# Moving key norms, token shift, decay mask and weight high parts between VectorE, ScalarE and TensorE in a two-layer trunk kernel

## The chip, the cores and the metric

One core of one Trainium2 chip runs the kernel. The metric is the device time of one execution in microseconds (us). Lower is better.

## The reference

A trunk of two layers over 512 tokens of width 1024, in fp32. Each layer is a mixer and then a SwiGLU feed-forward network (FFN), both behind an RMS norm and added to the residual stream. The first mixer ("even") has a short gated convolution and a gated delta rule with six heads of 128; the second ("odd") has an RWKV-7 scan with eight heads of 64, beside latent attention with eight heads. What the change touches is this:

```python
# even: gated delta rule in chunks
g = jnp.cumsum(to_chunks(g), axis=-1)
diff = g[..., :, None] - g[..., None, :]
decay = jnp.where(causal, jnp.exp(jnp.where(causal, diff, 0.0)), 0.0)
L = jnp.where(strict, jnp.einsum('bhncd,bhnsd->bhncs', kb, k) * decay, 0.0)
Tm = unit_lower_inverse(L)
...
# odd: token shift, key norm, RWKV-7 scan
z_rwkv = z + mu * (token_shift(z) - z)
r, k, v, wd, ad, gd = split_cols(z_rwkv, RWKV_SPLITS)
kk = l2_normalize((k * k_k).reshape(hshape))
k = k * (1.0 + (a - 1.0) * k_a)
y = rwkv7_scan(r_h, decay, k_h, v_h, kk, a)
```

## The kernel before

The order of the work is: even mixer (0 to about 267 us), its FFN (to 674), odd mixer (to 993), its FFN (to 1380). Activations lie with channels on the 128 partitions and the 512 tokens along the free dimension, in tiles of 128x512.

**Products.** To reach fp32 accuracy, weights and activations are split into a high part rounded to fp32r and a low part, and each product is three fp32r matmuls of 128x128 by 128x512. One projection of 1024 channels onto 128 is thus 24 matmuls into one PSUM bank. `weight` (line 340) loads a piece of a weight matrix, makes the high part (`hi`, by `self.copy`) and the low part (`lo`, raw minus high). A trace names these tiles `w`.

**Order of the work.** The program is a set of generators, one for each head, projection or convolution. A planner (`Plan`, `Engine`, `Core.run`) runs them against estimated costs and writes one instruction list for each engine; the chip then runs each list in its order. `self.copy` is put on ScalarE or VectorE and `E` on VectorE or GpSimd, whichever the planner expects to be done first. `A` is always ScalarE, `V` VectorE, `PE` TensorE. A generator takes a PSUM bank with `take("mx")` and gives it back with `rel("mx")`; the tags are `mx` (trace: mxps), `mm` (mmps) and `sc` (scps).

**Even mixer.** `even` projects queries, keys and values, convolves them with four taps (in the trace `x2k<-mmps,rs`, then one tap on ScalarE and three on VectorE, `conv_qkv`) and computes the gates: `gc`, the running sum of the log decay, and `gl`, its total. `decay(h)` makes for each head the mask matrix `dm` = exp(min(running sum - gc, mask)) of four chunks: four small matmuls of a broadcast gate column with the triangular `incl` put the running sums into a bank (trace: `mxps<-incl,g`), four VectorE instructions subtract `gc` and take the minimum with `negm` (0 or very negative), and ScalarE takes the exponential of all four, and that of the bank for `qT`. Each head's key product (`kT`) gives the squared key norms, through GpSimd (`R`) and VectorE (`rinv`), and then the matrix `L`. When all six heads have it, a blocked triangular inverse follows, mostly in series on VectorE (tile `big`), and then the scan over chunks on TensorE.

**Odd mixer.** `shifted(i, out)` (line 1260) multiplies a projection's bank by the RMS factor `rs` into `z`, gives the bank back, scales `z` by `omm` = 1 - mu and adds mu times `z` one token earlier. `keys(j)` (line 1504) serves two heads at a time, j = 0 to 3. It builds `ar[j]` (keys times decay, the first column of each 64-token chunk copied apart by VectorE, `ar<-x2k 128x8`) and `bk[j]`. The norms are summed on TensorE into `rn`, 128x8, by `TENSOR_SCALAR` and `RECIPROCAL`; VectorE copies `rn` out to 128x512 (`rb`, trace `x2k<-rn`) and four transposes put it into a bank, by which `kk0` is multiplied. Elsewhere `bk` is multiplied by `pcol`, and a blocked inverse like that of the even mixer works on tile `mem`. Attention follows, with its queries read back from memory (`f<-qd`), among early projections of the FFN.

Of the kernel before, what the change touches and what calls it, by code (L numbers as in the profile page):

```python
# [11 lines left out]
AF = mybir.ActivationFunctionType  # L12
# [4 lines left out]
T = 512  # L17
# [235 lines left out]
class Core:  # L253
# [86 lines left out]
    def weight(self, src, kt, m):  # L340

        n = kt * m
        part = lambda dt=F32R: self.tile(self.low, [128, 512], dt, "w", 12, typed=True)
        out = []
        for a in range(0, n, 512):
            w = min(512, n - a)
            if isinstance(src, tuple):
                hi, lo = part(), part()
                for t, x in zip((hi, lo), src):
                    self.dma(t[:, :w].bitcast(F32), x[:, a:a + w])  # L350
            else:
                raw, hi, lo = part(F32), part(), part()
                self.dma(raw[:, :w], src[:, a:a + w])
                self.copy(hi[:, :w], raw[:, :w])
                self.E.tensor_tensor(lo[:, :w], raw[:, :w], hi[:, :w], op=OP.subtract)
            out += [(hi[:, i:i + m], lo[:, i:i + m]) for i in range(0, w, m)]
        return out
# [170 lines left out]
    def rel(self, tag="mm"):  # L528
        self.held[tag] -= 1
# [138 lines left out]
    def even(self, gain, consts):  # L668
# [5 lines left out]
        with ExitStack() as ctx:  # L674
# [20 lines left out]
            betaf, gf = (t.rearrange("p h n -> p (h n)") for t in (beta, g))  # L695
            gc, gl = tl([U], "gc"), tl([U], "gl")
            neg_eg, e_gl, e_kd = tl([U], "neg_eg"), tl([U], "e_gl"), tl([U], "e_kd")
# [52 lines left out]
            def gates():  # L750
# [29 lines left out]
                PE.matmul(pg[:, U:2 * U], self.ones, gf, start=True, stop=True)  # L780
                V.tensor_copy(gc, pg[:, 0:U])
                V.tensor_copy(gl, pg[:, U:2 * U])
                rel("mx")
# [7 lines left out]
            def decay(h):  # L791
# [3 lines left out]
                for n in range(N):  # L795
                    u = h * N + n
                    PE.matmul(pb[:, blk(n)], gf[:, u:u + 1].to_broadcast([128, 128]), incl, start=True, stop=True)
                for n in range(N):
                    u = h * N + n
                    V.scalar_tensor_tensor(dm[:, u], pb[:, blk(n)], gc[:, u:u + 1], negm, op0=OP.subtract, op1=OP.min)  # L800
                A.activation(dm[:, h * N:(h + 1) * N], dm[:, h * N:(h + 1) * N], AF.Exp)
                A.activation(qT[:, h], pb, AF.Exp)
                rel("mx")
# [397 lines left out]
    def odd(self, xs, old, out):  # L1201
# [5 lines left out]
        with ExitStack() as ctx:  # L1207
# [52 lines left out]
            def shifted(i, out, ps=None, tag="mm"):  # L1260
# [4 lines left out]
                V.memset(z[:, 0:1], 0.0)  # L1265
                V.tensor_tensor(z[:, 1:T + 1], ps, rs, op=OP.mult)
                rel(tag)
                t = tmp()
                self.copy(t, z[:, 1:T + 1], omm[:, i:i + 1])
                V.scalar_tensor_tensor(out, z[:, 0:T], mu[:, i:i + 1], t, op0=OP.mult, op1=OP.add)  # L1270

# [232 lines left out]
            def keys(j):  # L1504
# [17 lines left out]
                E.tensor_tensor(ar[j][:, :, 0, 1:], ca[:, :, 1:], cE[:, :, 0:63], op=OP.mult)  # L1522
                V.tensor_copy(ar[j][:, :, 0, 0:1], ca[:, :, 0:1])
                V.scalar_tensor_tensor(kk0, th, 1.0, kk0, op0=OP.add, op1=OP.mult)
# [16 lines left out]
                V.reciprocal(rn, rn)  # L1541
                rb = tmp()
                V.tensor_copy(rb.rearrange("p (a c) -> p a c", c=64), rn[:, :, None].to_broadcast([128, 8, 64]))
                yield rb
                p = yield from take("mx")
                for n in range(4):
                    PE.transpose(p[:, blk(n)], rb[:, blk(n)], ident)
                V.tensor_tensor(kk0, kk0, p, op=OP.mult)
# [423 lines left out]
```

## Time and profile before

| what | value |
|---|---|
| median of three runs | 1370.57 us (1367.95 to 1374.75) |
| profiled execution, its own time | 1381.73 us |
| span of the profiled execution | 1380.0 us |
| TensorE busy | 1342.4 us (97%), 7526 records |
| VectorE busy | 850.9 us (62%) |
| ScalarE busy | 520.2 us (38%) |
| GpSimd busy | 365.6 us (26%) |
| chain of waits that ended last | TensorE 82%, VectorE 11%, DMA 3% |
| mean granted TensorE clock | 0.986 |

In the profile, PE is TensorE, DVE VectorE, ACT ScalarE and POOL GpSimd. One fp32r matmul is one record; an fp32 matmul is two records. The shares are means over stages that have different limits, so a stage's own stretch has to be looked at. The profiled execution took 0.8% more than the median.

### The profile page before, as it was taken

Reading aid. Unit: us, or ns where it says so; the run is one execution under the profiler, and the core shown is the slowest. Engines: PE = TensorE matmul, PEld = TensorE weight load, DVE = VectorE, ACT = ScalarE, POOL = GpSimd, SP = SyncE. Lnnn points to the kernel's source line nnn. Section 1 sums busy time; section 2 is a strip of 40 time slices with the busy share of each in tenths; the row PEclk is TensorE's granted clock in tenths of the full one; section 3 lists DMA queues with packets and bytes.
Section 4 is the critical chain, followed back from the end, with each engine's and each line's share of the span. In section 5 each row is a group of like instructions: output and inputs, shape, how many; then the busy total and the mean of one; then the engine's idle time right before and its main releaser. Section 6 shows DMA issues by size and latency. Waiting matters only on the chain.

```text
span 1380.0 us, 20285 instructions
## 1 busy us (share of the span) xinstructions
PE 1342.4 (97%) x7526; PEld 1080.5 (78%) x7526; DVE 850.9 (62%) x1598; ACT 520.2 (38%) x976; POOL 365.6 (26%) x367
## 2 busy tenths in 40 slices
PE   8988999999999999999989999999999999999998
PEld 5876888888887888888866777766788888888887
DVE  6999678657676555444398965656665443344432
ACT  5444464243233233334233144626544332233321
POOL 4454143225777766001122301430030000000000
PEclk9999899999999999999999999999999999999999
DMA  4222111256888987334623422475342333333332
GB/s 151 70 69 72 37 47 62 91 161 219 312 321 302 323 265 254 100 95 139 208 92 138 155 94 93 114 215 184 108 145 92 100 95 92 104 97 95 97 116 92
DMA packets 99939, 193.78 MB, mean 140 GB/s; under 512 B 13056, under 2 KB 21248, under 8 KB 99840
## 3 DMA queue, kind: packets, MB, share of 16 engines
q1 hardware_dynamic: 86976, 146.87, 33.5%
q0 software_dynamic: 12864, 45.62, 9.2%
q8 instruction: 59, 0.97, 0.3%
q14 instruction: 40, 0.33, 0.1%
HBM read 151.55 MB, written 40.89 MB: 139 GB/s over the span
## 4 chain that ended last, share of the span: by engine, by line
PE 82%; DVE 11%; DMA 3%; ACT 2%; issue 1%; POOL 1%; SPq 0%; DVEq 0%; POOLq 0%; ACTq 0%
PE mfps L390 56%; PE mmps L390 12%; PE mxps L390 10%; DVE x2k L242 3%; DVE big L242 3%; PE scps L390 2%; PE mxps L394 2%; DVE mem L242 1%; DVE ar L242 1%; DVE f L242 1%; DVE bk L242 1%; ACT mem L242 1%; DMA w<-in_w_oo 1%; DVE w L242 1%; SPq L318 0%
## 5 line engine op out<-in xcount | busy, mean ns | idle before, releaser
L390 PE MATMUL mfps<-big,w 128*128 128x512 f32 x3168 | 725.9, 389 | 0.0
L390 PEld LDWEIGHTS mfps<-big,w 128*128 128x128 f32 x3168 | 594.3, 188 | 123.7 <-DVE big L242 0.4
L242 DVE TENSOR_TENSOR w<-w,w 128x512 fp32r<-128x512 f32 (+1 forms) x318 | 253.4, 797 | 335.7 <-ACT w L242 325.7
L242 ACT ACTIVATE w<-w 128x512 fp32r<-128x512 f32 (+1 forms) x343 | 212.6, 621 | 462.1 <-DMA w<-in_w_gu 172.1
L390 PE MATMUL mmps<-big,w 128*128 128x512 f32 x936 | 246.9, 410 | 0.6 <-DVE x2k L242 0.6
L390 PEld LDWEIGHTS mmps<-big,w 128*128 128x128 f32 x936 | 172.4, 193 | 43.8 <-issue 7.0
L242 POOL TENSOR_TENSOR sqacc<-x2k,sqacc 128x512 f32<-128x512 f32 x21 | 28.1, 1339 | 236.8 <-ACT x2k L242 236.8
L242 POOL TENSOR_TENSOR slo<-sraw,shi 128x1024 fp32r<-128x1024 f32 (+1 forms) x36 | 74.2, 2062 | 14.6 <-DMA w_odl<-slo 12.3
L390 PE MATMUL mfps<-hid,w 128*128 128x512 f32 x288 | 71.6, 389 | 1.7 <-DVE hid L242 1.7
L390 PE MATMUL mxps<-big,w 128*128 128x512 f32 x288 | 73.2, 399 | 0.0
L242 POOL TENSOR_TENSOR w<-w,w 128x512 fp32r<-128x512 f32 x38 | 50.0, 1317 | 71.7 <-ACT w L242 38.2
L390 PEld LDWEIGHTS mfps<-hid,w 128*128 128x128 f32 x288 | 54.0, 188 | 13.4 <-DVE hid L242 2.2
L242 ACT ACTIVATE x2k<-x2k 128x512 f32<-128x512 f32 x61 | 38.5, 631 | 65.5 <-DVE x2k L242 52.2
L242 DVE TENSOR_TENSOR x2k<-mfps,rs 128x512 f32<-128x512 f32 x88 | 59.9, 683 | 3.1 <-PE mfps L390 2.6
L390 PEld LDWEIGHTS mxps<-big,w 128*128 128x128 f32 x288 | 52.2, 188 | 10.1 <-issue 0.2
L242 POOL CAST shi<-sraw 128x1024 fp32r<-128x1024 f32 (+1 forms) x36 | 35.2, 979 | 46.4 <-DMA w_odh<-shi 13.8
L242 DVE TENSOR_TENSOR x2k<-x2k,x2k 128x512 f32<-128x512 f32 x52 | 41.4, 798 | 4.6 <-ACT x2k L242 3.0
L394 PE MATMUL mxps<-c_ident,x2k 128*128 128x128 f32 (+1 forms) x182 | 31.2, 283 | 12.9 <-DVE x2k L242 9.8
L394 PEld LDWEIGHTS mxps<-c_ident,x2k 128*128 128x128 f32 (+1 forms) x182 | 20.8, 139 | 28.2 <-DVE x2k L242 16.7
L242 DVE TENSOR_TENSOR xres<-mfps,xres 128x512 f32<-128x512 f32 x32 | 22.0, 689 | 32.0 <-PE mfps L390 31.9
L242 ACT ACTIVATE x2k<-mxps 128x512 f32<-128x512 f32 (+4 forms) x60 | 26.5, 457 | 31.9 <-PE mxps L390 16.9
L242 DVE TENSOR_TENSOR big<-x2k,big 128x512 fp32r<-128x512 f32 x36 | 29.7, 824 | 5.0 <-ACT big L242 4.2
(367 smaller groups left out, 1432.9 us busy)
## 6 DMA issues: line engine op xcount, KB each, us to landing
w<-in_w_gu SPq DMA_DIRECT2D x176, 256.0 KB, 2.7
w<-in_w_down SPq DMA_DIRECT2D x64, 256.0 KB, 2.6
w<-in_w_ev SPq DMA_DIRECT2D x60, 256.0 KB, 2.7
sraw<-in_w_od POOLq DMA_DIRECT2D x20, 512.0 KB, 7.5
w_odh<-shi POOLq DMA_DIRECT2D x20, 512.0 KB, 3.7
w_odl<-slo POOLq DMA_DIRECT2D x20, 512.0 KB, 6.2
w<-w_odh SPq DMA_DIRECT2D x40, 256.0 KB, 2.8
w<-w_odl SPq DMA_DIRECT2D x40, 256.0 KB, 3.2
```

What stands on the lines that cost most here:

```text
L242: c.emit(t, lambda: getattr(eng, op)(*a, **kw))
L390: self.emit(t, lambda: self.nc.tensor.matmul(out, lhsT, rhs, **kw))
L394: self.emit(t, lambda: self.nc.tensor.transpose(out, x, ident))
```

## The change

- `weight`: the high part is always made by ScalarE.
- `decay(h)`: ScalarE first takes the exponential of the bank for `qT`; then TensorE adds the mask `negm` to the bank by one more matmul with the identity, over 512 columns; then ScalarE takes four exponentials with the bias `ngc` = -`gc`. The VectorE instructions are gone.
- `shifted`: ScalarE scales `z` into the projection's bank, VectorE adds the shifted product to it, and only then the bank is given back.
- `keys(j)`: the first column of `ar` is copied by ScalarE. The norms are spread by eight fp32 matmuls that take a column of `rn`, broadcast over 64, as weights and the identity as the moving operand, straight from `rn`.

```diff
@@ weight
-                self.copy(hi[:, :w], raw[:, :w])
+                self.A.activation(hi[:, :w], raw[:, :w], AF.Copy)
@@ even, gates
+                V.tensor_scalar(ngc, gc, -1.0, None, op0=OP.mult)
@@ even, decay(h)
-                    PE.matmul(pb[:, blk(n)], gf[:, u:u + 1].to_broadcast([128, 128]), incl, start=True, stop=True)
+                    PE.matmul(pb[:, blk(n)], gf[:, u:u + 1].to_broadcast([128, 128]), incl, start=n == 0, stop=n == N - 1)
+                A.activation(qT[:, h], pb, AF.Exp)
+                yield negm, self.clear(pb)
+                PE.matmul(pb, ident, negm[:, None, :].to_broadcast([128, N, 128]), start=False, stop=True, skip_group_check=True)
                 for n in range(N):
                     u = h * N + n
-                    V.scalar_tensor_tensor(dm[:, u], pb[:, blk(n)], gc[:, u:u + 1], negm, op0=OP.subtract, op1=OP.min)
-                A.activation(dm[:, h * N:(h + 1) * N], dm[:, h * N:(h + 1) * N], AF.Exp)
-                A.activation(qT[:, h], pb, AF.Exp)
+                    A.activation(dm[:, u], pb[:, blk(n)], AF.Exp, bias=ngc[:, u:u + 1])
                 rel("mx")
@@ odd, shifted
+                A.activation(ps, z[:, 1:T + 1], AF.Copy, scale=omm[:, i:i + 1])
+                V.scalar_tensor_tensor(out, z[:, 0:T], mu[:, i:i + 1], ps, op0=OP.mult, op1=OP.add)
                 rel(tag)
-                t = tmp()
-                self.copy(t, z[:, 1:T + 1], omm[:, i:i + 1])
-                V.scalar_tensor_tensor(out, z[:, 0:T], mu[:, i:i + 1], t, op0=OP.mult, op1=OP.add)
@@ odd, keys(j)
-                V.tensor_copy(ar[j][:, :, 0, 0:1], ca[:, :, 0:1])
+                A.activation(ar[j][:, :, 0, 0:1], ca[:, :, 0:1], AF.Copy)
@@ odd, keys(j)
-                rb = tmp()
-                V.tensor_copy(rb.rearrange("p (a c) -> p a c", c=64), rn[:, :, None].to_broadcast([128, 8, 64]))
-                yield rb
+                yield rn
                 p = yield from take("mx")
                 for n in range(4):
-                    PE.transpose(p[:, blk(n)], rb[:, blk(n)], ident)
+                    for i, b in enumerate(half):
+                        PE.matmul(p[b, blk(n)], rn[:, 2 * n + i:2 * n + i + 1].to_broadcast([128, 64]), ident, start=True, stop=True)
```

The planner works with other costs after this, so the lists shift in more places. VectorE's list has 1450 rows before and 1417 now. Three places, each before and now:

TensorE in the even mixer, where the gate sums (`incl`, `g`) of the first heads are made; scps_2859 before and scps_2843 now are the same projection's bank. Before:

```order
L390 MATMUL mxps_2860<-g_2805,incl_2802 128x24
L390 MATMUL mxps_2860<-g_2805,c_ones_2784 128x24
L390 MATMUL mxps_2861<-incl_2802,g_2805 128x128 x4
L390 MATMUL mxps_2829<-kT_2820 128x128 x4
L390 MATMUL mxps_2858<-incl_2802,g_2805 128x128 x4
L390 MATMUL mxps_2860<-incl_2802,g_2805 128x128 x4
L390 MATMUL scps_2859<-big_2827,w_2856 128x512
```

Now:

```order
L390 MATMUL mxps_2844<-g_2788,incl_2785 128x24
L390 MATMUL mxps_2844<-g_2788,c_ones_2767 128x24
L390 MATMUL mxps_2845<-incl_2785,g_2788 128x128 x4
L390 MATMUL mxps_2813<-incl_2785,g_2788 128x128 x4
L390 MATMUL mxps_2845<-negm_2786,c_ident_2766 128x512
L390 MATMUL mxps_2842<-kT_2804 128x128 x4
L390 MATMUL mxps_2844<-incl_2785,g_2788 128x128 x4
L390 MATMUL mxps_2813<-negm_2786,c_ident_2766 128x512
L390 MATMUL scps_2837<-kT_2804 128x128 x4
L390 MATMUL mxps_2844<-negm_2786,c_ident_2766 128x512
L390 MATMUL scps_2843<-big_2811,w_2840 128x512
```

Three of the six mask products stand here, ahead of the projection that before followed the gate sums; a second key product has come ahead of it too.

VectorE in the odd mixer, one pass of `keys` and what lies around it. Before:

```order
L242 TENSOR_TENSOR x2k_8354<-mmps_2844,rs_5602 128x512
L242 TENSOR_SCALAR x2k_8009<-x2k_8354,omm_8558 128x512
L242 SCALAR_TENSOR_TENSOR x2k_8289<-x2k_8354,od_mu_8552,x2k_8009 128x512
L242 TENSOR_SCALAR x2k_8155<-x2k_8289,od_vec_8553 128x512
L242 TENSOR_TENSOR f_8592<-x2k_8289,f_8592 128x512
L242 TENSOR_TENSOR ar_8591<-x2k_8155,f_8588 128x8x63
L242 COPY ar_8591<-x2k_8155 128x8
L242 SCALAR_TENSOR_TENSOR x2k_8155<-x2k_8222,x2k_8155 128x512
L242 TENSOR_TENSOR bk_8590<-f_8592,f_8585 64x8x64
```

Now:

```order
L242 TENSOR_TENSOR x2k_8142<-mmps_2828,rs_5589 128x512
L242 SCALAR_TENSOR_TENSOR x2k_8341<-x2k_8142,od_mu_8539,mmps_2828 128x512
L242 TENSOR_SCALAR x2k_8209<-x2k_8341,od_vec_8540 128x512
L242 TENSOR_TENSOR f_8579<-x2k_8341,f_8579 128x512
L242 TENSOR_TENSOR ar_8578<-x2k_8209,f_8575 128x8x63
L242 MEMSET x2k_8142 128x1
L242 SCALAR_TENSOR_TENSOR x2k_8209<-x2k_7996,x2k_8209 128x512
L242 TENSOR_TENSOR bk_8577<-f_8579,f_8572 64x8x64
```

The scaling by `omm` and the copy into `ar` are gone; the multiply by `rs` and the STT (SCALAR_TENSOR_TENSOR) that reads ScalarE's result stand next to each other; the STT that followed the copy follows a memset.

VectorE in the last stage of the even mixer's inverse. Before:

```order
L242 TENSOR_SCALAR big_2826<-scps_2853 32x12x32 x2
L242 TENSOR_TENSOR x2k_2833<-mxps_2829,rs_2855 128x512
L242 SCALAR_TENSOR_TENSOR mxps_2829<-x2k_2833,conv_qkv_2797,mxps_2829 128x512 x3
L242 COPY L_33_2823<-scps_2859 32x12x32
L242 COPY L_33_2823<-mxps_2860 32x12x32 x2
L242 COPY big_2826<-mxps_2860 32x12x32
```

Now:

```order
L242 TENSOR_SCALAR big_2810<-mxps_2813 32x12x32 x2
L242 TENSOR_TENSOR w_2865<-w_2882,w_2862 128x512
L242 COPY L_34_2807<-scps_2843 32x12x32
L242 COPY big_2810<-scps_2843 32x12x32
L242 COPY L_34_2807<-mxps_2845 32x12x32
L242 COPY big_2810<-mxps_2845 32x12x32
L242 TENSOR_TENSOR rv_2806<-mxps_2842,rinv_2800 128x512
L242 TENSOR_TENSOR x2k_2817<-mxps_2844,rs_2839 128x512
```

The copies out of PSUM into `L` and `big` have moved ahead of a convolution's multiply and its three taps.

## Rows read from the trace of the kernel before

**Rows 1.** Busy us by stretch: stretch, length, PE PEld DVE ACT POOL, PEclk, DMA share, GB/s

```profile
40.00:50.00 10.00, 10.00 (x54) 8.43 (x52) 9.64 (x37) 4.07 (x8) 4.06 (x4) 1.00 0.26 81
...
700.00:760.00 60.00, 54.23 (x283) 39.84 (x283) 53.50 (x86) 17.41 (x25) 13.71 (x8) 0.94 0.33 114
```

**Rows 2.** Timeline, PE and DVE from 70 us: start, us, engine line, operation, tiles, shapes

```profile
70.53 1.16 PE L390 MATMUL scps<-kT 128*128 128x128 f32 x8
71.45 8.90 PE L390 MATMUL mmps<-big,w 128*128 128x512 f32 x38
...
74.48 0.28 DVE L242 CUSTOM_DVE_ANT_0 junk<-scps,c_ident 128x128 f32<-128x128 f32 x1
```

**Rows 3.** Timeline, PE, an fp32 product over 512 columns (two records each)

```profile
897.90 3.60 PE L390 MATMUL mxps<-gd,c 128*128 128x512 f32 x8
```

**Rows 4.** Groups by form, DVE: count | busy us, mean ns | idle before, releaser

```profile
L242 DVE TENSOR_TENSOR w<-w,w 128x512 fp32r<-128x512 f32 x286 | 229.6, 804 | 300.9 <-ACT w L242 290.9 <-PE mmps L390 5.8 <-PE mfps L390 1.1
...
L242 DVE COPY ar<-x2k 128x8 f32<-128x8 f32 x4 | 7.8, 1938 | 0.0
L242 DVE SCALAR_TENSOR_TENSOR dm<-mxps,gc,negm 128x128 f32<-128x128 f32 x24 | 7.1, 343 | 0.0
...
L242 DVE TENSOR_SCALAR x2k<-x2k,omm 128x512 f32<-128x512 f32 x12 | 6.1, 511 | 0.4
...
L242 DVE CAST w<-w 128x512 fp32r<-128x512 f32 x13 | 5.5, 420 | 1.2 <-DMA w<-in_w_ev 1.2
...
L242 DVE COPY x2k<-rn 128x512 f32<-128x512 f32 x4 | 3.7, 932 | 0.1
...
L242 DVE COPY mem<-big 32x512 f32<-32x512 f32 x3 | 1.9, 640 | 0.1
...
L242 DVE TENSOR_TENSOR bk<-bk,pcol 128x1024 f32<-128x1024 f32 x1 | 1.2, 1217 | 0.0
```

**Rows 5.** Groups by form, ACT

```profile
L242 ACT ACTIVATE w<-w 128x512 fp32r<-128x512 f32 x311 | 195.8, 630 | 413.5 <-DMA w<-in_w_gu 172.1 <-DMA w<-in_w_down 78.9 <-DVE w L242 53.4
...
L242 ACT ACTIVATE mem<-big 32x512 f32<-32x512 f32 x5 | 5.8, 1161 | 2.2 <-DVE big L242 2.2
...
L242 ACT ACTIVATE vn<-mxps,br 128x128 f32<-128x128 f32 x14 | 5.1, 366 | 4.9 <-PE mxps L390 4.8
L242 ACT ACTIVATE mmps<-x2k,conv_qkv 128x512 f32<-128x512 f32 x7 | 4.8, 691 | 5.1 <-DVE x2k L242 5.0
```

**Rows 6.** Timeline, DVE, a convolution's second tap; brackets: idle before, releaser

```profile
26.02 0.76 DVE L242 SCALAR_TENSOR_TENSOR mmps<-x2k,conv_qkv,mmps 128x512 f32<-128x512 f32 x1 [0.84 <-ACT mmps L242]
```

**Rows 7.** Timeline, DVE and POOL, 692 to 712 us, around `ar` and `bk`

```profile
692.15 0.17 DVE L242 COPY ar<-x2k 128x8 f32<-128x8 f32 x1
...
694.24 1.70 DVE L242 SCALAR_TENSOR_TENSOR x2k<-x2k,x2k 128x512 f32<-128x512 f32 x1
...
708.72 3.14 DVE L242 COPY ar<-x2k 128x8 f32<-128x8 f32 x1
...
693.69 1.70 POOL L242 TENSOR_TENSOR bk<-f,f 64x512 f32<-64x512 f32 x1 [12.07 <-DVE f L242]
...
708.35 1.60 POOL L242 TENSOR_TENSOR bk<-f,f 64x512 f32<-64x512 f32 x1 [6.46 <-DVE f L242]
709.92 1.91 POOL L242 TENSOR_TENSOR bk<-bk,pcol 128x1024 f32<-128x1024 f32 x1
```

**Rows 8.** Timeline, PE, 716 to 759 us, the key norms' transposes and what follows

```profile
716.71 0.66 PE L394 MATMUL mxps<-c_ident,x2k 128*128 128x128 f32 x4 [1.57 <-DVE x2k L242]
...
719.28 8.02 PE L390 MATMUL mmps<-big,w 128*128 128x512 f32 x24
...
758.60 0.66 PE L394 MATMUL mxps<-c_ident,x2k 128*128 128x128 f32 x4 [1.98 <-DVE x2k L242]
```

**Rows 9.** Timeline, PE, attention: the wait for the queries, and 64-column weights

```profile
929.09 7.02 PE L390 MATMUL mxps<-f,f 96*128 96x128 f32 x14 [3.25 <-DMA f<-qd]
...
946.98 1.31 PE L390 MATMUL mxps<-x2k,f 128*64 128x128 f32 x20
```

More of the change, by code (lines that the diff above doesn't have):

```diff
@@ L695, in even @@
             betaf, gf = (t.rearrange("p h n -> p (h n)") for t in (beta, g))
-            gc, gl = tl([U], "gc"), tl([U], "gl")
+            gc, gl, ngc = tl([U], "gc"), tl([U], "gl"), tl([U], "ngc")
             neg_eg, e_gl, e_kd = tl([U], "neg_eg"), tl([U], "e_gl"), tl([U], "e_kd")
```

## The prediction

> **What bounds the kernel now.** I read the page's first part, then the busy time by stretches, then the chain of waits and the instruction lists of the stretches that the diff touches. Two facts carry the argument. In the even mixer's first 80 us TensorE has no gap (10.00 of 10 us between 40 and 50) while VectorE is nearly full beside it (9.64) [rows 1]. In the odd mixer VectorE is the bound: 53.50 of the 60 us from 700 to 760, with ScalarE at 17.41 and GpSimd at 13.71, and TensorE left 5.8 us idle at a mean granted clock of 0.94 [rows 1]. The two FFNs are TensorE streams that the change does not touch. So what leaves VectorE is worth much in the odd mixer and little in the even one, and what is added to TensorE before 80 us is paid.
>
> **Weights.** The 13 high-part casts that the planner had put on VectorE (420 ns each, 5.5 us) go to ScalarE at 630 ns, 8.2 us [rows 4, 5]. By the orders, 7 low-part subtractions come back from GpSimd to VectorE, 7 x 0.804 = 5.6 us [rows 4]. VectorE gains nothing; the 8.2 us lie in ScalarE's free time. I cost it at 0; if ScalarE had no room, up to 8 us would appear as TensorE waiting for weights.
>
> **Decay mask, even mixer.** Removed: 24 VectorE instructions of 343 ns, 8.2 us [rows 4]. Added: on ScalarE 24 exponentials over 128x128 from PSUM (366 ns for the like-shaped scaled copy [rows 5], 8.8 us) for six over 128x512; on TensorE six fp32 matmuls over 512 columns. The nearest such group is 8 records, four matmuls, in 3.60 us [rows 3]: 0.9 us each, 5.4 us in all, all in the stretch without gaps. A projection matmul costs 8.90/38 = 0.234 us [rows 2]. By the orders the last head's key product, which leads to the serial triangular inverse on VectorE, has 180 projection matmuls and the six mask products ahead of it, where it had 177: 3 x 0.234 + 5.4 = 6.1 us later. Against that, VectorE stood behind: it began reading that product at 74.48, 2.8 us after the product's end (70.53 + 1.16) [rows 2], and with 8.2 us taken off it this lag goes. So the inverse begins about 3 us later. In the inverse's last stage VectorE's new list reads three PSUM results before a convolution's multiply and three taps, instead of after (the order blocks of the section on the change): about 3 us back. Nine fewer projection matmuls stand ahead of the first scan product, so 9 x 0.234 = 2 us more follow in the TensorE-bound scan. Sum +2 us. Ends: +8 if neither lag nor reordering helps (6.1 + 2), -2 if VectorE's relief hides the matmuls altogether.
>
> **First column of the key operand, odd mixer.** Four VectorE copies of 128x8 take 7.8 us, 1938 ns each [rows 4]; one with no neighbour, at 692.15, took 0.17 [rows 7]. The others wait: the copy at 708.72 ends at 711.86, when a GpSimd multiply (708.35) and the one behind it (709.92 + 1.91 = 711.83) are done [rows 7]. That VectorE and GpSimd exclude each other is not the copy's peculiarity: the two-input STT at 694.24 took 1.70 us and ended at 695.94 beside a GpSimd multiply that ended at 695.39 [rows 7]. The next VectorE instruction after the removed copy is the same kind of STT, so the wait passes on to it. The planner moves two of the three `bk`-times-`pcol` multiplies (the second GpSimd instruction above) to VectorE, at 1.22 us [rows 4]: two waits fall from about 3 us to about 1.2, 3.6 us back, 2.4 paid, and 0.7 for the four copies themselves. I take -2. Ends: -5.4 (all waits gone, 7.8 less 2.4) and +1.7 (0.7 gained, 2.4 paid, no wait shorter).
>
> What the copy's row alone does not tell is whether its 3.1 us vanish with it. The Trainium skill, page "SBUF — State Buffer", section "SBUF: two separate sides", says that VectorE and GpSimd share a port pair as an exclusive lock, taken by VectorE for two-input or fast-mode work in SBUF, and that the later one blocks for the whole instruction. By this rule the wait is handed to the STT; read from the copy's row alone, 3.4 us more would go and the sum would be 3.4 us lower. The STT's row at 694.24 agrees with the rule.
>
> **Key norms, odd mixer.** Four broadcast copies of 128x512 leave VectorE, 3.7 us [rows 4]. TensorE waits for each of them, 1.57 us at 716.71 and 1.98 at 758.60 for two of the four [rows 8]; it would now wait only for the reciprocal before, so of these waits the copies' own time goes, 3.7 us at most, about 3. In return each group is 16 records over 64-column weights: 20 such took 1.31 us [rows 9], so 1.05, against 0.66 for four transposes [rows 8]: +0.4 each, +1.6 in all. After the wait at 716.71 the clock was low: 24 projection matmuls from 719.28 took 8.02 us, 0.334 each, 2.4 us more than at 0.234 [rows 8, 2]. These two sides overlap in time (VectorE's end is waited for by TensorE and then the other way), so I count one: -3.5. Ends: 0 and -7.5 (3.7 + 1.4 of TensorE + 2.4 of clock).
>
> **Shift, odd mixer.** Twelve VectorE scalings by `omm` of 511 ns go, 6.1 us [rows 4]; ScalarE scales into the product's bank instead, 691 ns like the first tap in the even mixer [rows 5]. VectorE then waits for it: there the tap waited 0.84 us from its multiply to its STT [rows 6], against 0.51 today. In VectorE's new order six of the shifts have nothing between multiply and STT: 6 x +0.33 = +2. Most of the others have one instruction between, which fills the wait, and keep roughly 0.35 us each: seven give -2.5. Sum -0.5; ends +3 (handoffs slower than in the even mixer) and -6 (every scaling gained).
>
> **Inverse in the odd mixer.** Two of three VectorE copies to `mem` (640 ns) go to ScalarE at 1161 [rows 4, 5], in a serial chain: +1.
>
> **Attention.** TensorE waits 3.25 us at 929.09 for a query transfer [rows 9]. In the new order 12 more projection matmuls stand before that point, 2.8 us of work that was due later. If the transfer keeps its time, -2.8; if it comes as much later, 0. I take -1.5.
>
> **Sum.** 0 + 2 - 2 - 3.5 - 0.5 + 1 - 1.5 = -4.5 us against the profiled execution's 1381.73, so 1377.2. That execution is 0.8% above the median of the runs, 1370.57; scaled by 1370.57/1381.73 the forecast is 1366.0. A measurement of this kernel can tell some 0.5%, 6.9 us, from no change: faster is below 1363.7, slower above 1377.4.
>
> **Rivals.**
> *Waits vanish.* The GpSimd lock does not reach the next STT in time, TensorE no longer idles near 716 and its clock stays up. Then the odd mixer gets -5.4 - 7.5 + 1 = -12 with the shift at 0, and with +2 and -1.5 the total is -11.5: 1359. For it: the waits of TensorE and the low clock are both there to be lost (0.94). Against: the row at 694.24. Chance 0.27.
> *No net change.* VectorE's freed time is filled by what the planner sends back to it and the next wait ends last: 1370.6. For it: the low-part subtractions and `bk` multiplies that return to VectorE. Against: VectorE's list still has 33 rows fewer. Chance 0.13.
> *ScalarE as middleman, slower.* All 14 shifts now pass through ScalarE's list, which also holds the inverse's copies of 1161 ns, seven instead of five. If a tap comes behind one, VectorE stands for it in the stretch that VectorE bounds: 14 x 1.16 = 16 us, less the 4.5, so +12, 1382. It decides from (4.5 + 6.9)/14 = 0.8 us of mean extra delay. Against: ScalarE is busy only 17.41 of 60 us there. Chance 0.10.
>
> **How the numbers follow.** The forecast has 0.50. Its own spread of some 5 us puts 0.15 of it below 1363.7 and 0.01 above 1377.4. Faster: 0.26 from the first rival and 0.15, 0.41. Slower: 0.10 and 0.01, 0.11. The same: 0.48. For 8 in 10 the range takes in the first rival with 3 us beyond it, 1356, and ends at 1377, short of the slower case.
>
> **What would show it.** Right: the inverse starting some 3 us later than 79.7; the STT behind the removed `ar` column taking over 1 us beside a GpSimd multiply; no TensorE wait over 1 us before the norm products; scalings gone but 0.8 us between multiply and STT. Wrong: an even mixer more than 6 us longer (mask products on the path, lag not recovered); odd stretch from 689 to its inverse shorter by over 8 us (waits vanished) or unchanged with ScalarE named as releaser (middleman); the FFNs' lengths changed at all.

## Result, and the profile after

The changed kernel takes 1383.03 us (median of 9 runs, 1379.80 to 1387.11), the kernel before, beside it, 1374.62 (9 runs, 1367.95 to 1379.65). The ratio is 1.0053 with a 95% interval of 1.0029 to 1.0076: slower by 0.5%, 7.3 us of 1374.62. The forecast was 1366.0 with a range of 1356 to 1377, so it failed; on the forecast's own base of 1370.57 the ratio gives 1377.8, outside the range as well.

I divided both profiled executions into stretches at starts that every trace shows: "even" ends where the first FFN's stream begins (the first long row of `mfps<-big,w`), "odd 1" runs from the end of that FFN's last product to the first product of the odd inverse (`mem,big`), "odd 2" from there to the second FFN's first product.

| us | before | changed | difference |
|---|---|---|---|
| even | 266.9 | 265.8 | -1.1 |
| first FFN | 406.7 | 409.3 | +2.6 |
| odd 1 | 134.8 | 133.1 | -1.7 |
| odd 2 | 184.8 | 190.3 | +5.5 |
| second FFN | 386.8 | 386.8 | 0 |
| span | 1380.0 | 1385.3 | +5.3 |

The loss is where I had expected a gain, in odd 2, the attention. The busy times by stretch of the changed kernel answer to [rows 1]; the last row is the stretch in which the loss lies:

```profile
40.00:50.00 10.00, 10.00 (x49) 7.80 (x49) 7.04 (x17) 4.10 (x9) 1.39 (x1) 1.00 0.25 79
...
700.00:760.00 60.00, 56.75 (x327) 43.41 (x327) 48.86 (x80) 22.88 (x36) 11.88 (x7) 0.94 0.33 114
945.00:960.00 15.00, 11.98 (x76) 7.86 (x73) 8.54 (x38) 7.72 (x20) 0.00 (x0) 0.89 0.25 86
```

Between 700 and 760 VectorE fell from 53.50 to 48.86 and TensorE's idle time from 5.8 to 3.3 us, as meant. Between 945 and 960 TensorE stands for 3.0 of 15 us although VectorE and ScalarE are busy for little more than half. What it waits for is in its timeline from 925 to 985 us (idle before the instruction and its releaser in brackets; waits under 1 us left out):

```profile
929.20 0.46 PE L390 MATMUL mxps<-f,f 96*128 96x128 f32 x2 [1.24 <-DMA f<-qd]
...
937.18 0.33 PE L394 MATMUL mxps<-c_ident,x2k 128*128 128x128 f32 x1 [1.50 <-ACT x2k L242]
...
949.97 0.33 PE L394 MATMUL mxps<-c_ident,x2k 128*128 128x128 f32 x1 [3.02 <-ACT x2k L242]
...
966.63 0.77 PE L394 MATMUL mxps<-c_ident,x2k 128*128 128x128 f32 x5 [1.98 <-ACT x2k L242]
```

The wait for the queries did shrink, from 3.25 us [rows 9] to 1.24. In its place come three waits for ScalarE's softmax, 6.5 us in all. ScalarE's timeline shows what stood ahead of those exponentials in its list:

```profile
935.17 0.63 ACT L242 ACTIVATE w<-w 128x512 fp32r<-128x512 f32 x1 [3.67 <-PE mxps L394]
...
948.32 0.63 ACT L242 ACTIVATE w<-w 128x512 fp32r<-128x512 f32 x1 [2.46 <-issue]
...
963.60 0.63 ACT L242 ACTIVATE w<-w 128x512 fp32r<-128x512 f32 x1 [1.86 <-issue]
```

These are casts, the making of the high parts, of weights for the odd mixer's output projection, the product that opens the stretch called second FFN. Each ends 1.0 to 2.4 us before the transpose that TensorE waited for, and ScalarE had stood for 1.9 to 3.7 us at each. (A fourth, at 981.32, cost it 0.96 us.) The chain of waits gives the order for the second:

```profile
943.25 2.62 DMA w<-in_w_oo
945.87 2.45 issue
948.32 0.04 ACT w L242
948.36 0.49 issue
948.86 1.06 ACT x2k L242 x3
949.92 0.04 issue
949.97 0.33 PE mxps L394
```

The weight's transfer, then the cast, then three softmax steps, then TensorE. The releasers named at these casts are not what they waited for. The trace keeps the landings of the transfers: the three `w<-in_w_oo` issued at 929.74, 943.25 and 960.07 landed at 935.10, 948.25 and 963.53, and each cast began 0.07 us later. The "issue" of 2.45 us is thus the rest of the transfer.

In the kernel before there were three such casts among the exponentials, not four, the first stood behind 11 exponentials, not two, and ScalarE stood long at that one only:

```profile
949.08 0.63 ACT L242 ACTIVATE w<-w 128x512 fp32r<-128x512 f32 x1 [2.23 <-DMA w<-in_w_oo]
...
960.28 0.63 ACT L242 ACTIVATE w<-w 128x512 fp32r<-128x512 f32 x1 [0.17 <-DMA w<-in_w_oo]
...
976.16 0.63 ACT L242 ACTIVATE w<-w 128x512 fp32r<-128x512 f32 x1 [0.22 <-DMA w<-in_w_oo]
```

The rest of the terms, in groups by form of the changed kernel (count | busy, mean ns | idle before, releaser):

```profile
L390 PE MATMUL mxps<-negm,c_ident 128*128 128x512 f32 x12 | 6.4, 619 | 1.4 <-ACT qT L242 1.4
L390 PE MATMUL mxps<-c_ident,rn 128*64 128x128 f32 x64 | 4.4, 279 | 2.1 <-DVE rn L242 2.1
...
L242 ACT ACTIVATE dm<-mxps,ngc 128x128 f32<-128x128 f32 x24 | 7.1, 370 | 3.3 <-PE mxps L390 3.3
L242 ACT ACTIVATE mmps<-x2k,omm 128x512 f32<-128x512 f32 x10 | 6.9, 692 | 22.1 <-DVE x2k L242 21.2 <-DMA w<-w_odh 0.8
...
L242 DVE SCALAR_TENSOR_TENSOR x2k<-x2k,od_mu,mmps 128x512 f32<-128x512 f32 x8 | 5.9, 742 | 5.4 <-ACT mmps L242 5.4
```

The prices were close: mask matmul 1.1 us a pair of records for 0.9, exponential 370 ns for 366, the shift on ScalarE 692 for 691, a group of norm products 1.09 us for 1.05. The last row is the shift's new wait.

### The profile page after: what moved, and what is told of

It is laid out like the page before. It is cut to its first block, busy times and chain, and to the rows that moved or that the text cites. A ratio compares the mean times of both kernels' runs of the same rounds, so it can differ in the third digit from the quotient of the medians.

```text
span 1385.3 us, 20418 instructions
## 1 busy us (share of the span) xinstructions
PE 1343.0 (97%) x7586; PEld 1080.1 (78%) x7586; DVE 839.5 (61%) x1540; ACT 546.1 (39%) x1032; POOL 351.5 (25%) x360
## 4 chain that ended last, share of the span: by engine, by line
PE 77%; DVE 12%; ACT 4%; DMA 3%; issue 2%; POOL 1%; SPq 1%; ACTq 0%; POOLq 0%; DVEq 0%
PE mfps L390 55%; PE mmps L390 12%; PE mxps L390 7%; DVE big L242 3%; DVE x2k L242 3%; PE scps L390 2%; PE mxps L394 1%; ACT x2k L242 1%; ACT mem L242 1%; DVE w L242 1%; DVE bk L242 1%; DVE f L242 1%; DMA w<-in_w_down 1%; DVE mem L242 1%; SPq L318 1%
## 5 line engine op out<-in xcount | busy, mean ns | idle before, releaser
L242 DVE TENSOR_TENSOR w<-w,w 128x512 fp32r<-128x512 f32 (+1 forms) x325 | 266.1, 819 | 331.4 <-ACT w L242 317.8
L242 ACT ACTIVATE w<-w 128x512 fp32r<-128x512 f32 x356 | 221.3, 623 | 472.8 <-DMA w<-in_w_gu 161.8
L390 PE MATMUL mxps<-big,w 128*128 128x512 f32 x240 | 62.5, 403 | 0.0
L390 PEld LDWEIGHTS mxps<-big,w 128*128 128x128 f32 x240 | 43.4, 188 | 9.7 <-issue 1.3
L242 POOL TENSOR_TENSOR w<-w,w 128x512 fp32r<-128x512 f32 x31 | 40.6, 1315 | 37.4 <-ACT w L242 22.8
L394 PE MATMUL mxps<-c_ident,x2k 128*128 128x128 f32 (+1 forms) x174 | 30.7, 288 | 11.7 <-ACT x2k L242 9.2
L242 ACT ACTIVATE x2k<-mxps 128x512 f32<-128x512 f32 (+4 forms) x53 | 23.7, 460 | 26.7 <-PE mxps L390 14.2
```

The lines of the kernel that those rows point to most:

```text
L242: c.emit(t, lambda: getattr(eng, op)(*a, **kw))
L390: self.emit(t, lambda: self.nc.tensor.matmul(out, lhsT, rhs, **kw))
L394: self.emit(t, lambda: self.nc.tensor.transpose(out, x, ident))
```

## Experiments

**Theory 1**: the loss is the order of the attention's lists. The planner puts 36 instead of 24 early projection matmuls ahead of the first query-key product, and with them the weights' transfers and casts fall elsewhere. **Theory 2**: ScalarE is overloaded by the operations it was given. **Theory 3**: the mask products on TensorE are paid. By the planner's lists only the shift and the key norms together give the changed kernel's attention order, called the late order; each alone gives a third order with 27 matmuls ahead. The edits below are shown by their telling lines.

All results in one table, by the stretches above (single profiles) and by the timed ratio to the kernel before. "Clock" is the mean granted TensorE clock from 130 to 170 us. The border between odd 1 and odd 2 does not part the same work in all runs: in e2, e6, e7 and e10 to e12 odd 1 also holds 12 narrow matmuls and (not in e6) 3 projection matmuls that elsewhere stand in odd 2. That is 2 to 3 us (1.91 us for the twelve in a row of the changed kernel, 3 x 0.234 for the others), so for these runs the sum of the two stretches is the safer number: 319.6 before, 323.4 changed, 313.0 in e2, 313.3 in e7, 311.8 in e9.

| run | clock | even | odd 1 | odd 2 | ratio (95%) |
|---|---|---|---|---|---|
| before | 0.83 | 266.9 | 134.8 | 184.8 | 1 |
| changed | 0.96 | 265.8 | 133.1 | 190.3 | 1.0053 (1.0029 to 1.0076) |
| e1 before, late order | 0.91 | 259.4 | 134.9 | 189.3 | 1.0040 (1.0011 to 1.0069) |
| e2 changed without shift | 0.96 | 264.7 | 129.7 | 183.3 | 0.9997 (0.9967 to 1.0026) |
| e3 mask alone | 0.91 | 262.9 | 133.0 | 186.9 | 1.0026 (1.0004 to 1.0048) |
| e4 shift and norms | 0.79 | 264.8 | 131.7 | 191.5 | 1.0020 (0.9989 to 1.0051) |
| e5 changed, attention as before | 0.91 | 264.7 | 133.1 | 186.8 | 1.0007 (0.9984 to 1.0031) |
| e6 shift alone | 0.83 | 264.6 | 132.4 | 183.7 | 0.9970 (0.9938 to 1.0003) |
| e7 norms and first column | 0.91 | 258.4 | 129.7 | 183.6 | 0.9933 (0.9907 to 0.9959) |
| e8 weights alone | 0.83 | 265.0 | 135.1 | 185.6 | 0.9981 (0.9958 to 1.0003) |
| e9 changed, casts on GpSimd | 0.96 | 264.0 | 133.2 | 178.6 | 0.9971 (0.9950 to 0.9993) |
| e10 weights, norms, first column | 0.96 | 258.7 | 129.6 | 185.1 | 0.9949 (0.9923 to 0.9976) |
| e11 e7, casts on GpSimd | 0.96 | 259.1 | 130.4 | 182.8 | 0.9962 (0.9933 to 0.9991) |
| e12 e10, casts on GpSimd, late order | 0.83 | 264.8 | 129.7 | 182.2 | 0.9948 (0.9919 to 0.9977) |
| e13 e9 without mask | 0.83 | 265.3 | 133.2 | 179.8 | 0.9934 (0.9907 to 0.9962) |

**e1, the order alone.** To the kernel before:

```diff
@@ early, after the projection
+                    if c == 2:
+                        done.add("e3")
                     V.tensor_tensor(x, ps, x, op=OP.add)
@@ attention, item
+                        yield ready("e3")
                         p = yield from take("qk")
```

> The kernel before, with one rule more for the planner: attention's first product waits until the third early projection has been listed. No operation is changed; the instruction lists of the attention come out in the changed kernel's order (36 early projection matmuls instead of 24 ahead of the first query-key product, four instead of three weight casts among ScalarE's softmax exponentials, the first of them in third place). Theory 1 (the loss is this order): slower than before by 4 to 8 us, all of it between the first query-key product and the second FFN, 69 us instead of 64. Theory 2 (ScalarE is overloaded by the operations it got) and theory 3 (the mask products on TensorE are paid): within 2 us of before, that stretch at 64.

1.0040 with the operations of the kernel before, odd 2 at 189.3. The loss of theory 1 can be had with no operation changed. It sits in another place, though, one wait ahead of the first product:

```profile
924.16 4.55 PE L390 MATMUL mmps<-big,w 128*128 128x512 f32 x10 [5.43 <-DMA w<-w_ool]
```

Here the third projection's weights came late. Behind the first product, where theory 1 had put all of the loss, the stretch took 61.6 us and not 69, although four casts stand among the exponentials. So the order can cost time, but this run does not show ScalarE's casts as the way.

**e2, the changed kernel without the shift** (`shifted` as before).

```diff
-                A.activation(ps, z[:, 1:T + 1], AF.Copy, scale=omm[:, i:i + 1])
+                self.copy(t, z[:, 1:T + 1], omm[:, i:i + 1])
```

> The changed kernel with the token shift as before (scaling on VectorE or by the planner's choice). The planner then lists 27 early projection matmuls ahead of attention, 3 more than before. Theory 1: faster than the changed kernel by 4 to 9 us, attention back to 63 to 66 us; at or below the time of before. Theory 2: faster than the changed kernel by 1 to 3 us, in the odd mixer before attention, since 14 of ScalarE's operations go. Theory 3: within 2 us of the changed kernel.

Odd 2 fell by 7.0 to 183.3 as theory 1 has it; odd 1 fell by 3.4 too, where only theory 2 expected a gain. With the 2 to 3 us of work that stand in odd 1 here, each stretch gained about 5 us: the shift costs time in both, in odd 2 by way of the order. That ScalarE's load is the reason in odd 1 is not shown.

**e3, the mask alone** (the three hunks in `even`).

```diff
+                A.activation(qT[:, h], pb, AF.Exp)
+                yield negm, self.clear(pb)
+                PE.matmul(pb, ident, negm[:, None, :].to_broadcast([128, N, 128]), start=False, stop=True, skip_group_check=True)
```

> The kernel before with only the decay mask changed. Attention has the order of before. Theory 1: within 3 us of before, even mixer 1 to 2 us shorter as in the changed kernel's trace. Theory 3: slower by 5 to 8 us, in the even mixer. Theory 2: within 2 us of before.

1.0026, 3.6 us slower: outside what theory 1 expected and short of theory 3, though the interval (0.6 to 6.6 us) reaches into both. Its odd 2, 186.9, is 2.1 above that of before with the same lists, which is how far single profiles of that stretch lie apart.

**e4, shift and norms together.**

```diff
+                A.activation(ps, z[:, 1:T + 1], AF.Copy, scale=omm[:, i:i + 1])
+                        PE.matmul(p[b, blk(n)], rn[:, 2 * n + i:2 * n + i + 1].to_broadcast([128, 64]), ident, start=True, stop=True)
```

> The kernel before with only the token shift and the key norms changed. These two together give the changed kernel's attention order, neither alone does. Theory 1: slower than before by 2 to 7 us: attention 69 us instead of 64, less what the odd mixer gains before it (1 to 3 us). Theory 2: within 3 us of before. Theory 3: faster than before by 1 to 5 us, since no mask product is there.

Odd 2 at 191.5, as in the changed kernel; with no mask the time is 1.0020, an interval that does not exclude 1. ScalarE stands at three casts as in the changed kernel (3.56, 1.79 and 1.69 us). Attention's loss needs no mask product, so theory 3 alone is out.

**e5, the changed kernel with the attention's order of before.**

```diff
@@ early
                 for c in range(KD):
+                    if c == 2:
+                        yield ready("att")
@@ attention, item, after the query-key product
+                        done.add("att")
```

> The changed kernel whole, with one rule more for the planner: the third early projection is not listed before attention's first query-key product. The attention's lists come out as those of the kernel before (24 early projection matmuls ahead, three weight casts among the exponentials). Theory 1 (order of the attention): faster than the changed kernel by 4 to 7 us; from the odd inverse's start to the second FFN 184 to 187 us, where the changed kernel had 190.3. Theory 2 (ScalarE overloaded): within 2 us of the changed kernel, that stretch at 189 or more.

1.0007 against 1.0053: three added lines that only reorder win back 0.46%, 6.3 us, with odd 2 at 186.8. This is theory 1's size, and the mask, the shift and ScalarE's load are all still in. ScalarE stands at two casts here too (3.73 and 2.10 us), but TensorE waits for ScalarE only 1.3 us in all from the first query-key product on, for 6.8 in the changed kernel. A cast at which ScalarE stands need not cost TensorE anything.

**e6, the shift alone.**

```diff
-                rel(tag)
-                t = tmp()
-                self.copy(t, z[:, 1:T + 1], omm[:, i:i + 1])
+                A.activation(ps, z[:, 1:T + 1], AF.Copy, scale=omm[:, i:i + 1])
```

> The kernel before with only the token shift through PSUM and ScalarE. Theory 1: the odd mixer up to its inverse within 2 us of before (133 to 135 us) by my sum of -0.5, and the stretch from there to the second FFN at 183 to 186 (27 early matmuls ahead of attention, as without the shift). Theory 2: the odd mixer up to its inverse longer than before by 2 us or more, since VectorE waits for ScalarE, and the time above before.

Odd 1 at 132.4, 2.4 below before and a little more than I expected; the timed interval still holds 1. In its profile the shift alone gains a little; beside the changes in `keys` odd 1 is 3.4 longer with it (e2).

**e7, both changes in `keys` alone.**

```diff
-                V.tensor_copy(ar[j][:, :, 0, 0:1], ca[:, :, 0:1])
+                A.activation(ar[j][:, :, 0, 0:1], ca[:, :, 0:1], AF.Copy)
-                yield rb
+                yield rn
```

> The kernel before with only the two changes in keys(j): first column by ScalarE, norms by TensorE from the 128x8 column. By my sum -2 and -3.5: the odd mixer up to its inverse 4 to 7 us shorter than before (128 to 131 us), the stretch behind it 183 to 186, the time 3 to 8 us below before. Theory 2: no gain beyond 2 us.

As expected in both stretches: odd 1 5.1 shorter, odd 2 183.6. The time is 0.67% faster (1366.62 us), 9.2 us by the ratio, a little beyond the 8 expected. The lock's wait did pass on. In the kernel before, the STT behind the copy of 3.14 us in [rows 7] was short:

```profile
711.97 0.69 DVE L242 SCALAR_TENSOR_TENSOR x2k<-x2k,x2k 128x512 f32<-128x512 f32 x1
```

VectorE's and GpSimd's timelines in e7, without the copy:

```profile
698.91 3.36 DVE L242 SCALAR_TENSOR_TENSOR x2k<-x2k,x2k 128x512 f32<-128x512 f32 x1 [0.21 <-ACT ar L242]
...
698.25 1.59 POOL L242 TENSOR_TENSOR bk<-f,f 64x512 f32<-64x512 f32 x1 [11.77 <-DVE f L242]
699.81 1.91 POOL L242 TENSOR_TENSOR bk<-bk,pcol 128x1024 f32<-128x1024 f32 x1
```

The STT ends at 702.27. Copy and STT together had taken 3.83 us (3.14 + 0.69); the STT alone now takes 3.36. The Trainium skill, page "SBUF — State Buffer", section "SBUF: two separate sides", calls the pair of ports that VectorE and GpSimd share an exclusive lock held for a whole instruction. This STT waited through two GpSimd instructions (to 701.72), which agrees.

**e8, the weights alone.**

```diff
-                self.copy(hi[:, :w], raw[:, :w])
+                self.A.activation(hi[:, :w], raw[:, :w], AF.Copy)
```

> The kernel before with only the weights' high parts always on ScalarE. All theories: within 2 us of before, by my sum 0; ScalarE 3 us busier and VectorE the same within 3 us. If casts on ScalarE are the cause of the loss (theory 2 in its narrow form): slower by 4 us or more.

0.9981 with an interval that holds 1: nothing that can be told from 0, as forecast. The rule that the casts go to ScalarE is not what hurts; the casts in the attention were ScalarE's before the change too.

**e9, the late casts on GpSimd.** To the changed kernel:

```diff
@@ mixer_out
+                c.cast_on_g = l == 1
                 ps = c.do(c.project(w[k], ys, kt=len(ys), tag="mf", late=k < 2))
+                c.cast_on_g = False
@@ weight
+                if getattr(self, "cast_on_g", False):
+                    self.G.tensor_copy(hi[:, :w], raw[:, :w])
+                else:
+                    self.A.activation(hi[:, :w], raw[:, :w], AF.Copy)
```

> The changed kernel whole, with the high parts of the second FFN's first eight weight pieces (output projection, eight instructions) made by GpSimd, which is idle in the attention, instead of ScalarE. TensorE's list is the same; ScalarE's loses the four casts that stand among the softmax exponentials and wait for their transfers. Theory 1a (the loss in attention is ScalarE standing at those casts): odd inverse to second FFN 184 to 187 us instead of 190.3, 3 to 6 us faster than the changed kernel. Theory 1b (the early projections are used up and TensorE has nothing to fill the softmax's waits): within 2 us of the changed kernel.

This settles the place. TensorE's list is the changed kernel's, 36 matmuls ahead and all; odd 2 is 178.6, 11.7 less, and the time 0.82% less (1.0053 to 0.9971), about twice what I expected. TensorE's waits from 920 to 985 us (waited for: us in total, times, longest; the rows of TensorE's matmuls only):

```profile
PE mfps L393 <- DVE big L242: 1.5, 1, 1.5
...
PE mxps L397 <- DVE x2k L242: 0.8, 1, 0.8
...
PE mxps L393 <- DMA f<-qd: 0.6, 1, 0.6
PE mmps L393 <- DMA w<-w_ool: 0.4, 1, 0.4
PE mxps L393 <- DVE x2k L242: 0.3, 1, 0.3
```

No wait for ScalarE is left, and TensorE lacks no work: theory 1b falls. GpSimd stands idle instead, 4 to 13 us ahead of each cast, and no engine waits for it:

```profile
941.69 0.61 POOL L242 CAST w<-w 128x512 fp32r<-128x512 f32 x1 [11.15 <-DVE x2k L242]
...
965.06 0.62 POOL L242 CAST w<-w 128x512 fp32r<-128x512 f32 x1 [13.07 <-DMA w<-in_w_oo]
```

Not all of the 11.7 us is waiting. From the first query-key product on TensorE's waits shrank by 7.8 us (9.9 to 2.1) and its busy time by 4.1 (59.2 to 55.1) for the same work. That is its clock. In the changed kernel it fell to half, 1.2 GHz, behind two of the waits for ScalarE; these are its busy times by stretch, with the granted clock third from the end:

```profile
950.60:954.00 3.40, 3.40 (x22) 2.51 (x21) 1.91 (x9) 1.81 (x5) 0.00 (x0) 0.50 0.00 0
967.60:971.00 3.40, 3.40 (x18) 2.34 (x18) 1.43 (x6) 1.30 (x4) 0.00 (x0) 0.50 0.24 84
```

In e9 the granted clock is 1.00 from the first query-key product to the second FFN.

**e10, weights and keys.**

```diff
@@ weight, keys(j)
+                self.A.activation(hi[:, :w], raw[:, :w], AF.Copy)
+                A.activation(ar[j][:, :, 0, 0:1], ca[:, :, 0:1], AF.Copy)
+                yield rn
```

> The kernel before with the weights' high parts on ScalarE and the two changes in keys(j); no decay mask, no shift. The sum of the single runs: 0.993 x 0.998 of before, 1363 to 1368 us. If the weights' change costs something beside the others: 1369 or more.

1366.02 us, within what was expected; the weights add nothing to the keys.

**e11, keys with the late casts on GpSimd** (e7 with the edit of e9).

```diff
+                c.cast_on_g = l == 1
```

> The kernel before with the two changes in keys(j), and with the eight late casts on GpSimd as above. Theory 1a: 1 to 3 us below the keys' changes alone (ScalarE stood 3.2 us at the first of three such casts there), odd inverse to second FFN 181 to 183 us instead of 183.7. Theory 1b: no difference beyond 1 us.

Odd 2 fell by 0.8 only, less than theory 1a had, and the time did not fall (0.9962, its interval overlaps e7's). In this order the casts stand where they cost little: of the orders run, it is the changed kernel's in which they hurt.

**e12, the late order without shift and mask** (e10 with the edits of e1 and e9).

```diff
+                        yield ready("e3")
+                c.cast_on_g = l == 1
```

> Weights and both changes in keys(j), the eight late casts on GpSimd, and attention's first product only after the third early projection, as in the first experiment; no mask, no shift. Theory 1a: with no cast in ScalarE's way the early projections ahead of attention are a gain: odd inverse to second FFN 178 to 182 us, the time 1356 to 1364. If the forced order waits for its weights as in the first experiment (5.4 us): 183 to 186 there, 1362 to 1369.

Odd 2 is 182.2, just above the first bound, with 2 to 3 us of work fewer in it than in e9; the time, 1367.56 us, is in the second bound and not below e10. The lists are not quite those of the changed kernel, and short waits for weights, 1.1 us in all, stand among them; forcing the order gains nothing here.

**e13, e9 without the mask.**

```diff
-                    A.activation(dm[:, u], pb[:, blk(n)], AF.Exp, bias=ngc[:, u:u + 1])
+                    V.scalar_tensor_tensor(dm[:, u], pb[:, blk(n)], gc[:, u:u + 1], negm, op0=OP.subtract, op1=OP.min)
```

> The changed kernel with the decay mask as before and the eight late casts on GpSimd; beside the ninth experiment it has only the mask fewer. By my sum for the mask (+2, ends -2 and +8): 0 to 5 us faster than the ninth. Theory 3 in what is left of it (the mask products are paid in full): 5 to 8 us faster, in the even mixer. If the mask gains: slower.

1364.69 us (1361.31 to 1376.54), 0.9934 of before. From 0.9971 to 0.9934 is 5.1 us: with e3's 3.6 the mask costs some 4 us. The intervals of e9 and e13 overlap, so the size is no better known than to a few us. Its profile cannot show it, since its even mixer ran at the low clock (265.3 at 0.83). With e7 this is the fastest version; the kernel before and the changed one are both slower.

## Why the prediction was wrong, point by point

*Attention, -1.5: the step that failed.* I counted 12 matmuls moved into TensorE's wait and let the worst case be no gain at all. I looked at TensorE's list and its transfer, and not at what the other engines' lists hold in that place. The wait did shrink, from 3.25 to 1.24 us, between the two cases that I had priced. But ScalarE's casts had moved ahead among the exponentials, ScalarE stood 3.67, 2.46 and 1.86 us there for their transfers, TensorE waited 6.5 us behind it, and odd 2 grew by 5.5. With the casts off ScalarE odd 2 is 178.6 (e9), below the 184.8 of before. How much of that is the 12 matmuls' and how much the casts' is not shown: no run has the order of before with its casts on GpSimd.

*Mask, +2: too small.* The mechanisms that I named for the inverse's start came. The last key product came 5.2 us later (75.75 for 70.53, forecast 6.1), VectorE's lag behind it fell from 2.8 to 1.0 us, and the inverse began at 81.89, 2.2 later than in the profile of before for a forecast of 3. (That profile is the latest of ten without the mask's change; in the nine others the inverse begins at 76.8 to 78.3.) The 24 removed instructions overlap, so their row in [rows 4] has 7.1 us of busy time and not the 8.2 that I counted; and TensorE stood 1.4 us for `qT` ahead of the first mask product, which I had not priced. In the changed kernel:

```profile
75.75 1.05 PE L390 MATMUL mxps<-kT 128*128 128x128 f32 x8
...
77.77 0.28 DVE L242 CUSTOM_DVE_ANT_0 junk<-mxps,c_ident 128x128 f32<-128x128 f32 x1
...
81.89 4.44 DVE L242 COPY big<-L 32x768 f32<-32x768 f32 x3
```

What I mis-sized is the work put off into the scan, 9 projection matmuls by my count. I took it at the first product that belongs to the scan; at the first product with the state `S` (before and changed below) 399 projection matmuls have gone for 429, so 30 x 0.234 = 7.0 us more follow in a stretch nearly without gaps (0 and 0.7 us).

```profile
168.56 0.39 PE L390 MATMUL mxps<-S,kT 128*128 128x128 f32 x2
```

```profile
158.48 0.39 PE L390 MATMUL scps<-S,kT 128*128 128x128 f32 x2
```

With the changed mask the stretch from that product to the FFN takes 107.3 us (265.8 - 158.5), without it 98.3 (266.9 - 168.6), and the inverse before it is shorter by less: 76.6 us (158.5 - 81.9) against 82.6 in e7, whose clock there was as good (0.96 for 0.93). In profiles with a clock of 0.91 or more from 130 to 170, the even mixer takes 258.4 to 259.4 without the mask's change (e1, e7, e10, e11) and 262.9 to 265.8 with it (the changed kernel, e2, e3, e5, e9): +3.5 at least, where the timed runs give some 4. All five profiles with the change have that clock, six of the ten without it a lower one; whether the change keeps the clock up, and so gives part of its cost back, no run tests. The single profile of before had hidden the cost. It ran that part at 0.83, the changed one at 0.96:

```profile
130.00:170.00 40.00, 36.44 (x452) 30.75 (x451) 26.66 (x53) 18.46 (x38) 6.99 (x8) 0.83 0.11 34
```

```profile
130.00:170.00 40.00, 37.75 (x492) 31.73 (x491) 29.86 (x61) 23.34 (x52) 7.66 (x8) 0.96 0.16 48
```

The first row is the kernel before, the second the changed one.

*First column -2 and key norms -3.5: right in the ways, if anything too small.* Together -5.1 in odd 1 and -6.3 over both odd stretches (e7), -9.2 timed (5.6 to 12.8), by the ways given: the lock's wait passed on to the STT, two `bk` multiplies went to VectorE, and TensorE's four waits for the broadcast copy became one for `rn`, 1.7 us. Beside these the granted clock of odd 1 rose from 0.97 to 1.00, which I had left out as an overlap. *Inverse, +1: not seen.* TensorE's waits for ScalarE's `mem` are 1.3 us before and in the changed kernel; no run takes this term alone.

*Shift -0.5: wrong sign beside the keys.* The handoff was priced well (six waits of 0.69 to 0.8 us, one of 1.97, 7.3 in all) against 6.1 us of scalings saved. But ten instructions wait, not six: an instruction between multiply and STT fills the wait in part only. The 3.4 us in odd 1 (133.1 to 133.2 in the changed kernel, e5, e9 and e13; 129.6 to 130.4 in e2, e7, e10, e11 and e12, with more work in it) are more than the 1.2 that this gives, and alone the shift even gains 2.4. In the traces the difference lies at TensorE. In odd 1 of the changed kernel it waits 4.6 us, in e2 2.4. It waits for `bk` at 743.63, and from 745.8 to 752.6 its clock is at half, 1.2 GHz; e2 has neither. The wait in the changed kernel:

```profile
743.63 4.58 PE L390 MATMUL mxps<-ar,bk 64*128 64x128 f32 x32 [1.10 <-DVE bk L242]
```

The stretch around it, first in the changed kernel, then in e2 (granted clock third from the end):

```profile
740.00:760.00 20.00, 18.90 (x93) 15.22 (x92) 14.35 (x23) 3.56 (x7) 2.92 (x2) 0.83 0.34 119
```

```profile
740.00:760.00 20.00, 20.00 (x120) 15.98 (x120) 17.73 (x31) 1.02 (x3) 2.89 (x2) 1.00 0.42 138
```

Which handoff makes `bk` late no run takes apart.

*Weights 0: right* (e8). *The first FFN's +2.6* is in the changed kernel's single profile: at 442.00 TensorE waits 2.62 us, for 1.73 before, and its clock is at half until 445.4. e9, with the same lists there, has 406.2.

The sum by what the runs showed: mask +4, odd 1 -5.1 + 3.4, attention +5.5, weights 0, together +8, for 7.3 measured. It mixes timed ratios with single profiles, so that it comes this close is partly luck. The *slower rival* named ScalarE as the middleman in front of which others stand, and gave 1382; the sign is right, but its place was wrong: the shift's handoffs cost 7.3 us over 14 steps, short of its 0.8 us of mean extra delay, and the largest loss came from ScalarE's casts in the attention. *Waits vanish* came by half in e7: the clock of odd 1 stayed up and one wait over 1 us was left ahead of the norm products, but the lock's wait passed on. *No net change* did not come.

## What to carry to other kernels

When a change moves work ahead into a wait, look at the same place in every engine's list, not only in the one that waits: an instruction that depends on a transfer and stands in an in-order list ahead of a latency chain stops that chain, however small it is. Put such instructions on an engine that nobody waits for there; here eight casts of 0.6 us moved to an idle engine were worth 0.8% in the changed kernel's order, and nothing that could be measured in e7's. And where a planner sets the order, judge an edit with the order held fixed: three lines that only reorder were worth nearly the whole difference measured (e5).

## What the runs showed that I had not expected

- The even mixer's time goes with the clock granted from 130 to 170 us. Without the mask's change it took 258.4 to 259.4 us in four profiles at 0.91 or more and 264.6 to 266.9 in six at 0.79 to 0.83. Each group has runs with the lists of before and with those that the weights' change shifts a little. One profile of each kernel does not compare this stage.
- Two small edits that are neutral or better alone (the shift 0.9970; the norms, timed with the first column, 0.9933) gained nothing together (1.0020, an interval that holds 1). Only both together turned the planner to the late order.
- GpSimd made a 128x512 high part in 0.61 us, as fast as ScalarE's 0.63.
